# Band attention with a second pair of transposed weight tiles, a fourth row tile and a third query tile

## The chip, the cores and the metric

The kernel runs on one core of a Trainium2 chip. The time is the device time of one execution in microseconds, the median of three runs. A core has five engines that work side by side, each through its own queue in order: TensorE (PE, matmuls and transposes, with its weight loads shown apart as PEld), VectorE (DVE), ScalarE (ACT), GpSimd (POOL) and SyncE (SP), which here issues all the transfers. SBUF is the on-chip memory with 128 partitions, PSUM the banks that TensorE writes into.

## The reference

One step of a streaming encoder layer, on 2048 prompt tokens and 32 sample tokens of width 1024, in float32:

```
z = rmsnorm(x) @ w_in            # queries, keys, values of groups A and B
A: differential attention, 4 heads, two score maps each, all earlier chunks
B: band attention, 8 heads of 64: each 64-token chunk sees itself and 8 chunks before it
   s = q k^T / 8 + bias(head, distance); p = softmax(s); o = p v
h = x + concat(norm(A), norm(B)) @ w_out
h = h + relu(rmsnorm(h) @ w_up)^2 @ w_down
h = h + sigmoid(h @ w_ple_gate) * (p @ w_ple_proj)
y = rmsnorm(h)
```

The new keys and values are outputs too. The change concerns group B, the band attention.

## The kernel before

Every large product is made of three matmuls: each operand is split into a high part and a low part (`split`: a copy to the high part, and raw minus high for the low part), and `mm3` adds high x high, high x low and low x high. Weights come in units of 512 KB (`wunit`): one load (`wr`), a copy on ScalarE (`wh`, L169) and a subtraction on GpSimd (`wl`, L164).

The tokens are handled in four blocks of 512 (the last has the 32 sample tokens with it). In the order of the program `run` does: normalisation and group A's projections for blocks 0 and 1; group A's attention for their queries; group B's projections of blocks 0 and 1 with the normalisation of 2 and 3; band attention for the first 1024 queries; group B's projections of blocks 2 and 3; band attention for the other 1024 and the sample; group A's projections of blocks 2 and 3; group A's attention for those; and then, by blocks, output projection, MLP, gate and final normalisation. The order in which instructions really stand on each engine is not written out. The framework lays it out from priorities (program order, mostly) and a modelled time of each instruction. An instruction can be placed once its inputs are there and the tile that it writes has been released. So work from later in the program fills the holes of work before it: in the profile the projections of group A run within the first half of the band attention, and the output projection and MLP of block 0 within the second half.

A tile comes from a pool under a tag, with `bufs` copies. The tile of the next round waits until one copy has been released by its last reader. SBUF pools lie on two stacks, one from below (left), one from above (right). The band attention's pool `b` is on the right and is opened before its first half and closed after its second.

`attn_b` goes over four groups of query pairs, two in each half (`JB`), and in each over the eight heads. For each head and group it loads the head's bias (`bb`), keys (`kbt`) and values (`vbt`), each with two copies, and calls `attn_b_pair` for every pair of 128-query tiles, or for the sample's 32 queries (a visit, in what follows). One visit does, with L for a line of the kernel:

- `load_q`: two loads of 128 KB into the query tile `q` (two copies);
- for each of the two query tiles, scores `sb` in PSUM (L726) over up to 640 keys, bias and row maximum on VectorE into the row tile `eb` (tag `e`, three copies, L729; the small numbers are in `stb`), the exponential on ScalarE (L734), the reciprocal of the sum (L735), and the scaling on ScalarE (L736);
- transposes of the row tile into PSUM `tpb` (L741), a copy on ScalarE to the high part `pHb` (L750), and the low part `pLb` on VectorE (L751). Each holds both query tiles of the visit, and there is one copy of each;
- value matmuls `ob` (L766), the sum of the two halves of `ob` (L771 and L772), and the store to `oT`.

Three PSUM banks hold scores, two hold transposes, one holds the output.

Of the kernel before, what the change touches and what calls it, by code (L numbers as in the profile page):

```python
# [12 lines left out]
F32 = mybir.dt.float32  # L13
F32R = mybir.dt.float32r
# [5 lines left out]
P = 128  # L20
# [113 lines left out]
class Kern:  # L134
# [364 lines left out]

    def load_q(self, pool, gi, t0, n, maps):  # L500
        nc = self.nc
        q = pool.tile([P, len(maps), 2, 256], F32R, tag="q", bufs=2, name="q")
        for d in range(2):
            for i, m in enumerate(maps):
                self.dma(
                    q[64 * d : 64 * d + 64, i, :, :n],
                    self.qS[gi, :, 64 * m : 64 * m + 64, t0 : t0 + n].rearrange("l r c -> r l c"),
                )
        return q
# [182 lines left out]
    def attn_b_pair(self, h, j, kt, v, kb, bb, pool, ps_s, ps_t, ps_o):  # L692
        nc = self.nc
        gi, m = 4 + h // 2, h % 2
        samp = j is None
        if samp:
            tiles, t0, nq = [None], SP, SS
        else:
            tiles, t0, nq = [2 * j, 2 * j + 1], 256 * j, 256
        q = self.load_q(pool, gi, t0, nq, (m,))  # L700
        kfirst = 0 if samp else max(0, 2 * j - 4)
        pH = pool.tile([P, 6, 256], F32R, tag="pH", bufs=1, name="pHb")
        pL = pool.tile([P, 6, 256], F32R, tag="pL", bufs=1, name="pLb")
        spans = []
        for qi, t in enumerate(tiles):
            if samp:
                nr, k0, n, b0 = SS, SP, PAST + SS, 384
                kts = [(0, P), (1, SS)]
            else:
                nr = P  # L710
                f = max(0, t - 4)
                k0, n = P * f, P * (t + 1 - f)
                b0 = 640 - n
                kts = [(i, P) for i in range(f, t + 1)]
            spans.append(kts)
            if n <= 512:
                nb, w = 1, n
            else:
                nb, w = 2, n // 2
            e = pool.tile([P, 640], F32, tag="e", bufs=3, name="eb")[:nr, :n]  # L720
            st = pool.tile([P, 5], F32, tag="st", bufs=3, name="stb")[:nr]
            for i in range(nb):
                s = ps_s.tile([P, 512], F32, tag="s", name="sb")[:nr, :w]
                for hl in range(2):
                    c = k0 - kb + w * i
                    nc.tensor.matmul(  # L726
                        s, q[:, 0, hl, P * qi : P * qi + nr], kt[:, c : c + w], start=hl == 0, stop=hl == 1
                    )
                nc.vector.tensor_tensor_reduce(  # L729
                    e[:, w * i : w * i + w], s, bb[:nr, b0 + w * i : b0 + w * i + w], 1.0, -3e38,  # L730
                    ALU.add, ALU.max, st[:, 3 + i : 4 + i],
                )
            nc.vector.tensor_reduce(st[:, 0:1], st[:, 3 : 3 + nb], axis=AX.X, op=ALU.max, negate=True)
            nc.scalar.activation(e, e, AF.Exp, bias=st[:, 0:1], accum_out=st[:, 1:2])  # L734
            nc.vector.reciprocal(st[:, 2:3], st[:, 1:2])  # L735
            nc.scalar.activation(e, e, AF.Copy, scale=st[:, 2:3])  # L736
            for x0 in range(0, len(kts), 4):
                ch = kts[x0 : x0 + 4]
                tp = ps_t.tile([P, 4, P], F32, tag="tp", name="tpb")
                for x, (i, kn) in enumerate(ch):  # L740
                    nc.tensor.transpose(  # L741
                        tp[:kn, x, :nr], e[:, P * (x0 + x) : P * (x0 + x) + kn], self.ident[:nr, :nr]
                    )
                groups = [(0, len(ch), P)] if not samp else [(0, 1, P), (1, 1, SS)]
                for a0, na, kn in groups:
                    sl = ch[0][0] - kfirst + a0
                    h_ = pH[:kn, sl : sl + na, P * qi : P * qi + nr]
                    l_ = pL[:kn, sl : sl + na, P * qi : P * qi + nr]
                    s_ = tp[:kn, a0 : a0 + na, :nr]
                    nc.scalar.activation(h_, s_, AF.Copy)  # L750
                    nc.vector.tensor_tensor(l_, s_, h_.bitcast(F32), op=ALU.subtract)  # L751
        o = ps_o.tile([P, 256], F32, tag="o", name="ob")
        order = []
        if samp:
            order = [(0, P, 0, nq), (1, SS, 0, nq)]
        else:
            s0 = [i for i, _ in spans[0]]
            s1 = [i for i, _ in spans[1]]
            both = [i for i in s0 if i in s1]
            order = [(i, P, 0, 256) for i in both]  # L760
            order += [(i, P, 0, 128) for i in s0 if i not in s1]
            order += [(i, P, 128, 256) for i in s1 if i not in s0]
        for x, (i, kn, qa, qb) in enumerate(order):
            vt = v[:kn, (SP - kb) // P + i] if samp else v[:kn, i - kb // P]
            for y, pt in enumerate((pH, pL)):
                nc.tensor.matmul(  # L766
                    o[:, qa:qb], vt, pt[:kn, i - kfirst, qa:qb],
                    start=x == 0 and y == 0, stop=x == len(order) - 1 and y == 1,
                )
        t1 = pool.tile([64, 256], F32, tag="t1", bufs=2, name="t1")[:, :nq]  # L770
        nc.scalar.activation(t1, o[64:128, :nq], AF.Copy)  # L771
        nc.vector.tensor_tensor(t1, o[0:64, :nq], t1, op=ALU.add)  # L772
        self.dma(self.oT[64 * m : 64 * m + 64, gi, t0 : t0 + nq], t1)
# [532 lines left out]
```

## Time and profile before

| | |
|---|---|
| runs | 3271.13, 3277.6, 3279.51 us; median 3277.6 |
| profiled execution | 3282.74 us, its span 3281.0 us |
| mean granted TensorE clock | 0.974 |
| TensorE busy | 3096.6 us, 94% of the span |
| ScalarE, GpSimd, VectorE busy | 1696.1, 1711.0, 1562.2 us |
| memory traffic | 149 GB/s over the span |

How to read it: a row of a table of stages has, for a stretch of the span, the busy time of each engine with the count of its instructions, and then the clock that TensorE was granted (1.00 is full speed), the mean busy share of the 16 DMA engines, and what they moved in GB/s. A row of waits names who waited, for whom, the total in us, how often, and the longest. A row of instructions has line, engine, operation, output and inputs, shape and count, then busy time, the mean of one in ns, and the idle time of the engine before them with what ended it. Buffer numbers are left out of names. Some matmul records may be missing, and ends of matmuls are modelled.

### The profile page before, as it was taken

To read this page: it belongs to the slowest core of one execution; us is meant where nothing else is said; L and a number is where in the kernel's file an instruction comes from. 1 tells how busy PE (TensorE), PEld (TensorE's weight loads), DVE (VectorE), ACT (ScalarE), POOL (GpSimd) and SP (SyncE) were. 2 spreads that over 40 slices of the span, in tenths; PEclk is the share of its full clock that TensorE was granted. 3 is DMA by queue.
4 is the path that set the end of the run, shared out by engine and by line. 5 is a ranking of instruction groups with operands and counts; after the bars stand their busy time and mean duration, and the time that the engine had idled before them with its cause. 6 is when DMAs were issued, how large, how long until landed. Compare 5 with 4: busy or idle time off the path is not lost.

```text
span 3281.0 us, 51609 instructions
## 1 busy us (share of the span) xinstructions
PE 3096.6 (94%) x17881; PEld 2713.4 (83%) x17881; DVE 1562.2 (48%) x3952; ACT 1696.1 (52%) x3717; POOL 1711.0 (52%) x2515
## 2 busy tenths in 40 slices
PE   6998999899989999999999999998989999999998
PEld 6877788899877888778788877877779999999988
DVE  5116786444455544566655655735442232223235
ACT  4226676666656766666665656744442222222245
POOL 5436776433335544656654644676954333333377
PEclk9998999999999999999999999999989999999999
DMA  7488886876778654545655355357531111111123
GB/s 230 169 258 241 226 246 199 230 225 199 221 210 240 166 140 120 159 137 152 195 136 142 109 139 139 111 159 227 164 102 49 46 46 50 45 48 46 46 91 106
DMA packets 519085, 489.03 MB, mean 149 GB/s; under 512 B 37884, under 2 KB 414016, under 8 KB 518824
## 3 DMA queue, kind: packets, MB, share of 16 engines
q1 hardware_dynamic: 518824, 485.73, 50.8%
q8 instruction: 142, 2.33, 0.3%
q14 instruction: 119, 0.97, 0.1%
HBM read 379.06 MB, written 110.49 MB: 149 GB/s over the span
## 4 chain that ended last, share of the span: by engine, by line
PE 54%; DMA 5%; DVE 4%; POOL 2%; ACT 1%; issue 1%; SPq 0%; DVEq 0%; POOLq 0%; ACTq 0%
PE dps L190 7%; PE ups L191 7%; PE ups L190 7%; PE ups L192 7%; PE dps L192 7%; PE dps L191 7%; PE s L567 2%; PE gps L190 1%; PE gps L191 1%; DMA ka<-kS 1%; PE gps L192 1%; PE tpp L639 1%; POOL wl L164 1%; DMA wr<-w_up 1%; PE ob L766 1%
## 5 line engine op out<-in xcount | busy, mean ns | idle before, releaser
L164 POOL TENSOR_TENSOR wl<-wr,wh 128x256 fp32r<-128x256 f32 x936 | 690.9, 770 | 501.1 <-ACT wh L169 473.0
L971 DVE TENSOR_TENSOR h<-h,dps 128x512 f32<-128x512 f32 (+1 forms) x640 | 373.1, 585 | 597.5 <-PE dps L192 584.9
L169 ACT ACTIVATE wh<-wr 128x1024 fp32r<-128x1024 f32 x338 | 356.9, 1056 | 581.0 <-PE dps L191 285.7
L154 POOL TENSOR_TENSOR wl<-wr,wh 128x256 fp32r<-128x256 f32 x416 | 305.0, 764 | 407.0 <-ACT wh L169 403.7
L190 PE MATMUL dps<-uh,wh 128*128 128x512 f32 (+1 forms) x1280 | 458.6, 358 | 10.1 <-DVE h L971 5.5
L190 PE MATMUL ups<-cH,wh 128*128 128x512 f32 (+1 forms) x1280 | 453.3, 354 | 9.9 <-ACT relu L936 5.0
L191 PE MATMUL ups<-cL,wh 128*128 128x512 f32 (+1 forms) x1280 | 452.9, 354 | 4.1 <-DVE cL L175 3.6
L192 PE MATMUL ups<-cH,wl 128*128 128x512 f32 (+1 forms) x1280 | 453.2, 354 | 0.0
L191 PE MATMUL dps<-ul,wh 128*128 128x512 f32 (+1 forms) x1280 | 451.0, 353 | 0.0
L192 PE MATMUL dps<-uh,wl 128*128 128x512 f32 (+1 forms) x1280 | 450.9, 353 | 0.0
L154 POOL TENSOR_TENSOR ul<-relu,uh 128x136 fp32r<-128x136 f32 (+1 forms) x320 | 201.7, 652 | 167.7 <-ACT uh L169 166.4
L190 PEld LDWEIGHTS ups<-cH,wh 128*128 128x128 f32 x1280 | 242.8, 190 | 42.3 <-ACT relu L936 5.3
L190 PEld LDWEIGHTS dps<-uh,wh 128*128 128x128 f32 x1280 | 242.5, 189 | 42.4 <-DVE h L971 9.0
L191 PEld LDWEIGHTS ups<-cL,wh 128*128 128x128 f32 x1280 | 243.3, 190 | 36.0 <-DVE cL L175 3.8
L192 PEld LDWEIGHTS dps<-uh,wl 128*128 128x128 f32 x1280 | 242.0, 189 | 33.7
L192 PEld LDWEIGHTS ups<-cH,wl 128*128 128x128 f32 x1280 | 243.1, 190 | 30.1
L191 PEld LDWEIGHTS dps<-ul,wh 128*128 128x128 f32 x1280 | 242.2, 189 | 26.2
L190 PE MATMUL qps<-aH,wh 128*128 128x512 f32 (+1 forms) x640 | 231.3, 361 | 8.6 <-ACT kr L432 3.4
L191 PE MATMUL qps<-aL,wh 128*128 128x512 f32 (+1 forms) x640 | 229.6, 359 | 0.0
L192 PE MATMUL qps<-aH,wl 128*128 128x512 f32 (+1 forms) x640 | 228.9, 358 | 0.0
L567 PE MATMUL s<-ka,q 128*128 128x256 f32 (+4 forms) x784 | 190.4, 347 | 26.6 <-DMA ka<-kS 10.9
L581 ACT ACTIVATE e<-s,nm 128x512 f32<-128x512 f32 (+3 forms) x256 | 155.1, 611 | 68.7 <-DVE nm L573 46.0
(218 smaller groups left out, 7118.3 us busy)
## 6 DMA issues: line engine op xcount, KB each, us to landing
wr<-w_up SPq DMA_DIRECT2D x96, 512.0 KB, 4.2
wr<-w_down SPq DMA_DIRECT2D x96, 512.0 KB, 3.7
wr<-w_in SPq DMA_DIRECT2D x74, 512.0 KB, 5.2
q<-qS SPq DMA_DIRECT2D x256, 128.0 KB, 4.2
v<-vSa SPq DMA_DIRECT2D x64, 512.0 KB, 4.0
ka<-kS SPq DMA_DIRECT2D x32, 512.0 KB, 7.7
wr<-w_out SPq DMA_DIRECT2D x32, 512.0 KB, 5.4
wr<-w_ple_gate SPq DMA_DIRECT2D x32, 512.0 KB, 4.3
```

Of the source, the lines that this page charges most:

```text
L154: nc.gpsimd.tensor_tensor(out[:, sl], a[:, sl], b[:, sl], op=op)
L164: nc.gpsimd.tensor_tensor(out[:, sl], a[:, sl], b[:, sl], op=op)
L169: nc.scalar.activation(hi, raw, AF.Copy)
L190: nc.tensor.matmul(ps, lh, rh, start=start and i == 0, stop=False)
L191: nc.tensor.matmul(ps, lh, rl, start=False, stop=False)
L192: nc.tensor.matmul(ps, ll, rh, start=False, stop=stop and i == n - 1)
L567: nc.tensor.matmul(s, q[:, m, hl, P * qi : P * qi + nr], kt[:, m, k0 : k0 + n], start=hl == 0, stop=hl == 1)
L581: nc.scalar.activation(dst, src, AF.Exp, bias=nmx, accum_out=z[:nr, m, bi : bi + 1])
L639: nc.tensor.transpose(tp[:kn, x, :nr], w[:nr, P * i : P * i + kn], self.ident[:nr, :nr])
L766: nc.tensor.matmul(o[:, qa:qb], vt, pt[:kn, i - kfirst, qa:qb], start=x == 0 and y == 0, stop=x == len(order) - 1 and y == 1,)
L971: nc.vector.tensor_tensor(hv, hv, ps, op=ALU.add)
```

## The change

Four counts of tile copies and one size are changed; no instruction is added or taken away. In the band attention the query tile has three copies (in group A's attention, which passes two maps, it stays at two), `pHb` and `pLb` have two copies each, and `e` and `st` four. The program sets aside 1024 bytes of each SBUF partition for descriptors of dynamic DMAs, in place of the default 16384; they lie at address 0, below the left stack.

```diff
     def load_q(self, pool, gi, t0, n, maps):
         nc = self.nc
-        q = pool.tile([P, len(maps), 2, 256], F32R, tag="q", bufs=2, name="q")
+        q = pool.tile([P, len(maps), 2, 256], F32R, tag="q", bufs=4 - len(maps), name="q")
...
-        pH = pool.tile([P, 6, 256], F32R, tag="pH", bufs=1, name="pHb")
-        pL = pool.tile([P, 6, 256], F32R, tag="pL", bufs=1, name="pLb")
+        pH = pool.tile([P, 6, 256], F32R, tag="pH", bufs=2, name="pHb")
+        pL = pool.tile([P, 6, 256], F32R, tag="pL", bufs=2, name="pLb")
...
-            e = pool.tile([P, 640], F32, tag="e", bufs=3, name="eb")[:nr, :n]
-            st = pool.tile([P, 5], F32, tag="st", bufs=3, name="stb")[:nr]
+            e = pool.tile([P, 640], F32, tag="e", bufs=4, name="eb")[:nr, :n]
+            st = pool.tile([P, 5], F32, tag="st", bufs=4, name="stb")[:nr]
...
-    nc = bacc.Bacc("TRN2", target_bir_lowering=False, num_devices=1)
+    nc = bacc.Bacc("TRN2", target_bir_lowering=False, num_devices=1, dynamic_dma_scratch_size=1024)
```

## The prediction

> **What bounds the kernel now.** I read the page's busy times, its chain and its queues first, then a table by stages, then the waits inside the stage that the change touches. TensorE comes first on the page:
>
> ```profile
> PE 3096.6 (94%) x17881; PEld 2713.4 (83%) x17881; DVE 1562.2 (48%) x3952; ACT 1696.1 (52%) x3717; POOL 1711.0 (52%) x2515
> PE 54%; DMA 5%; DVE 4%; POOL 2%; ACT 1%; issue 1%; SPq 0%; DVEq 0%; POOLq 0%; ACTq 0%
> q1 hardware_dynamic: 518824, 485.73, 50.8%
> ```
>
> TensorE works for 3096.6 of 3281.0 us. The change adds and removes no instruction, so the TensorE work stays. What can move is its idle time, 184 us in all, and the clock it is granted. Band attention runs from 603 to 1330 us (its value matmuls, quoted further down). The stages, with the clock, the DMA share and GB/s in the last three columns:
>
> ```profile
> core 0: us, PE busy (x) PEld busy (x) DVE busy (x) ACT busy (x) POOL busy (x), PEclk, DMA share, GB/s
> 590.00:1340.00 750.00, 707.44 (x4282) 623.68 (x4281) 361.43 (x1237) 472.35 (x983) 307.04 (x486) 0.98 0.68 192
> 590.00:900.00 310.00, 289.90 (x2071) 271.38 (x2069) 141.65 (x548) 195.82 (x442) 101.44 (x182) 0.97 0.76 220
> 900.00:1000.00 100.00, 85.83 (x430) 70.95 (x431) 53.86 (x152) 61.98 (x118) 39.43 (x58) 0.93 0.75 210
> 1000.00:1340.00 340.00, 331.71 (x1782) 281.35 (x1781) 165.92 (x538) 214.56 (x424) 166.16 (x247) 1.00 0.58 162
> 300.00:500.00 200.00, 182.97 (x1088) 161.04 (x1086) 152.00 (x464) 136.49 (x391) 147.52 (x208) 0.94 0.82 230
> 200.00:250.00 50.00, 39.98 (x209) 33.54 (x209) 10.53 (x33) 13.48 (x29) 18.85 (x29) 0.89 1.03 320
> 2450.00:3100.00 650.00, 650.00 (x4038) 590.46 (x4037) 172.03 (x330) 182.69 (x316) 253.14 (x400) 1.00 0.15 46
> ```
>
> In the band stage, 590 to 1340 us, TensorE idles 750 - 707.4 = 42.6 us, and a clock of 0.98 costs about 15 us more (2% of 750): 57.6 us, 7.7% of the stage. Its parts differ: 20.1 us idle in the first half, 14.2 us in the hundred microseconds after it, 8.3 us in the last 340. The reason is the filler: projections in the first half, the MLP in the last, while after 900 us the projections have run out. The late MLP alone (2450 to 3100) keeps TensorE at 100%. So band attention is not slow work that stands in the way. It is a chain of small steps between which other work is fitted, and only the holes count. Which waits make them:
>
> ```profile
> PE sb L726 <- DVE stb L729: 10.4, 13, 3.6
> PE sb L726 <- DMA q<-qS: 5.9, 5, 1.8
> PE ob L766 <- ACT pHb L750: 4.6, 3, 2.3
> PE ops L190 <- DVE hd L860: 3.9, 2, 3.5
> PE tpb L741 <- DVE pLb L751: 1.7, 3, 0.8
> ```
>
> **What the single pair of weight tiles holds back.** One head of the second half, in which two pairs of query tiles and then the sample's 32 queries are done, from the time lines of ScalarE and TensorE (start, length, instruction):
>
> ```profile
> 1203.50 0.41 ACT L736 ACTIVATE eb<-eb,stb 32x160 f32<-32x160 f32 x1
> 1204.97 0.60 ACT L750 ACTIVATE pHb<-tpb 128x512 fp32r<-128x512 f32 x1
> ...
> 1218.68 0.27 PE L766 MATMUL ob<-pLb,vbt 128*128 128x128 f32 x1
> 1218.88 0.27 PE L741 MATMUL tpb<-ident,eb 32*128 32x32 f32 x2
> 1219.55 0.20 ACT L750 ACTIVATE pHb<-tpb 128x32 fp32r<-128x32 f32 x1
> ```
>
> The sample's row of 160 keys is scaled and ready at 1203.9 us. At 1205.0 a pair of prompt tiles begins to fill `pHb`, and its last value matmul ends at 1218.95. Only then is the sample transposed (1218.88) and copied (1219.55). It has waited 15 us, with one of three `e` tiles in its hands. With one `pHb`/`pLb` the pairs pass in single file, and the order in which the instructions are laid out puts filler between them.
>
> **The change, part by part.**
>
> Second `pHb`/`pLb` pair: the copies of one pair may run while the last one's value matmuls are pending. Waits at stake on TensorE: `ob` on `pHb` 4.6 and `tpb` on `pLb` 1.7 us. Bounds: from -6.3 (both go) to +6.3 (the copies queue on a busier ScalarE and both double). I take -4.6: the first goes, the second is a bank of PSUM, which the change leaves alone. Late next is the score bank (`sb` behind `stb`).
>
> Third query tile: two loads of 128 KB for each visit, started one visit earlier. No load is added.
>
> ```profile
> q<-qS SPq DMA_DIRECT2D x130, 128.0 KB, 3.7
> SPq L145 <- PE sb L726: 35.6, 23, 4.7
> SPq L145 <- POOL wl L164: 42.4, 24, 6.0
> ```
>
> SP, which issues every transfer in order, stood 35.6 us behind `sb` matmuls that still read a query tile or keys, and all later loads, the weight loads among them, stood behind it. A landing takes 3.7 us, less than a visit (a band of 727 us over 64 pairs and 8 sample visits, 10 us). So the 5.9 us that TensorE waited for queries should go: -5.9, with 0 as the other end if SP is held by `wl` (42.4 us, which the change doesn't touch).
>
> Fourth `e` and `st`: two prompt pairs hold four. Waits at stake are `sb` behind `stb`, 10.4 us; this is VectorE draining score banks, of which there are three as before. From -10.4 to +10.4; I take 0, because a tile for the result doesn't free a bank.
>
> The gap from 900 to 1000 us: 14.2 us idle, 3.6 and 3.5 us of it in the two longest single waits above. With more rows in flight, attention can fill part of it. Bounds 0 and -14.2; I take a third, -5.
>
> Scratch: 15,360 bytes of each partition come free at address 0, the left-hand pools slide down by that, and 2,048 + 2 x 6,144 + 2,560 + 20 = 16,916 bytes are taken on the right. No instruction hangs on it; the work that would show a cost is the next stage's start, whose tiles lie where the band pool lay, before as after: 0. [...]
>
> Clock: 15 us lost against 42.6 idle is 0.35 us for each idle microsecond. 4.6 + 5.9 + 5 = 15.5 less idle gives -5.5. Bounds 0 and -15. [...]
>
> What denser attention costs: first, how far ScalarE lets it be denser. Two rows for the instructions on `eb` on ScalarE, one for those on `pHb` on all engines, and the groups of the output:
>
> ```profile
> 590.00:900.00 310.00, 100.85 (x207) 0.97 0.76 220
> 900.00:1340.00 440.00, 109.54 (x201) 0.98 0.62 173
> 603.00:1330.00 727.00, 88.87 (x352) 68.84 (x352) 104.17 (x238) 91.29 (x238) 0.98 0.67 191
> L771 ACT ACTIVATE t<-ob 64x256 f32<-64x256 f32 x64 | 24.4, 381 | 40.7 <-PE ob L766 37.8 <-DMA q<-qS 1.7
> L766 PE MATMUL ob<-pHb,vbt x352: 178/281/562, 603.3 to 1329.8; 128*128 128x256 f32 x120, 128*128 128x128 f32 x48, 128*128 128x32 f32 x8
> ```
>
> ScalarE's part is 100.85 + 109.54 on `eb`, 91.29 (the fourth time of the third row) on `pHb`, and 24.4 for the output: 210.4 + 91.3 + 24.4 = 326 us of ScalarE for attention, in a band of 727 us, and 472 with the filler's. If nothing but ScalarE held it, the band would take 472 us. I take the middle of 727 and 472, 600 us. Filler displaced from it runs later, where it costs TensorE its own time and no more (2450 to 3100). But in a denser stage TensorE waits oftener: from 300 to 500 us, with VectorE at 76% and ScalarE at 68%, it loses 17.0 us idle and 12 us of clock, 14.5%. I charge +8 us, about a quarter, since VectorE is the slacker engine here, between 0 and the +30 that the rival below works out.
>
> Sum: -4.6 - 5.9 - 5 - 5.5 + 8 = -13 us. The profiled execution took 3282.7 us (3281.0 span and 1.7 around it), 5.1 above the median of 3277.6. It becomes 3269.7, and the median 3264.6: 3265 us.
>
> **The rivals.**
>
> Slower, by density. The stage is 600 us long and loses at the rate of 300 to 500 us: 600 x 14.5% = 87 us, against 57.6 now: +30, 3308 us. It decides from 57.6 / 600 = 9.6% on. For it: the last 340 us lose only 2.4% in idle while ScalarE runs at 63%; there is hardly anything to win there and much to lose. Against it: from 300 to 500 VectorE was the busier engine, and the band leaves VectorE at 48%. Chance 0.31.
>
> Slower, by transfers. The first half moves 220 GB/s at a DMA share of 0.76. Packed from 310 into 250 us it needs 0.94. At 1.03 (200 to 250 us) TensorE idled 20%. A hundred microseconds of that are 20 us, less the 6.5 those lose now: +14, 3292 us. It decides once the share passes that of 300 to 500 us, 0.82, for long. Chance 0.08.
>
> Slower, by the scratch. The page calls the queue dynamic, and if its descriptors did lie in the scratch, transfers would land later, a query tile say as late as the slowest loads on the page:
>
> ```profile
> ka<-kS SPq DMA_DIRECT2D x32, 512.0 KB, 7.7
> ```
>
> That is 4.0 us more for each landing. TensorE's five waits for queries would grow by 5 x 4.0 = 20 us: 3298. It decides from about 3 us more per landing. Chance 0.03.
>
> No change to be measured: TensorE is full, and what attention gives up filler takes. Within 0.3% (10 us, about what a measurement here tells from nothing): 3278. Chance 0.10.
>
> **How the numbers follow.** Forecast 0.48; so faster 0.48, same 0.10, slower 0.31 + 0.08 + 0.03 = 0.42. The forecast's own range is 3240 to 3268. The low end of the whole range takes the idle 42.6 us and 5 us of clock away: 3230. The high end is the density rival at 650 us, 94 - 57.6 = +37: 3315.
>
> **What would show it.** Right: the last `ob` ends near 1200 us, not 1330; the copies into `pHb` begin before the last pair's value matmuls end; TensorE's waits for queries are nearly gone; the sample's row no longer waits 15 us; the next attention stage starts and ends earlier by as much; TensorE's idle total falls from 184 to about 170 us. The density rival would show ScalarE above 75% in the band with more `sb` behind `stb`; the transfers, waits for `kbt`, `vbt`, `bb` with the share above 0.9. What makes it wrong: a new order of instructions that opens holes elsewhere, above all where the MLP ends and the output projection starts.

## The result, and the profile after

The changed kernel takes 3262.46 us (median of 19 runs, 3251.43 to 3271.29), the kernel before 3278.56 us beside it (19 runs, 3270.78 to 3292.62). The ratio is 0.9948, with a 95% interval of 0.9937 to 0.9958: faster by 0.5%, some 17 us. The profiled execution took 3256.5 us, 6 us less than the median, and the profiled one of before was 4 us above its own. So the spans of the two profiles, 3281.0 and 3254.6 us, lie 26 us apart, about 10 us of which is chance.

The page's lines on busy time and on the chain, after:

```profile
PE 3076.7 (95%) x17881; PEld 2692.7 (83%) x17881; DVE 1557.3 (48%) x3952; ACT 1693.7 (52%) x3717; POOL 1706.8 (52%) x2515
PE 26%; DVE 1%; ACT 0%; issue 0%; DVEq 0%; POOL 0%; POOLq 0%
```

The counts of instructions are the same. TensorE's idle time is 3254.6 - 3076.7 = 177.9 us, 6.5 less than before's 184.4.

The table of stages, after, with the same columns as in the prediction:

```profile
590.00:1340.00 750.00, 714.95 (x4361) 627.76 (x4360) 392.91 (x1309) 494.78 (x1055) 306.54 (x484) 0.99 0.69 197
590.00:900.00 310.00, 289.83 (x2082) 268.00 (x2081) 154.80 (x615) 211.98 (x479) 90.92 (x169) 0.99 0.77 223
900.00:1000.00 100.00, 94.13 (x538) 80.64 (x537) 60.20 (x169) 65.46 (x129) 47.10 (x69) 0.98 0.84 242
1000.00:1340.00 340.00, 330.99 (x1745) 279.12 (x1745) 177.90 (x527) 217.35 (x448) 168.51 (x248) 0.99 0.58 160
2450.00:3100.00 650.00, 650.00 (x4040) 590.07 (x4039) 179.07 (x344) 179.99 (x310) 251.84 (x397) 1.00 0.16 48
```

The late MLP is as full as it was. The band stage idles 35.0 us in place of 42.6. All of that is the hundred microseconds after 900: 5.9 idle, down from 14.2. The first half (590 to 900 us: 20.2 against 20.1) and the last 340 us (9.0 against 8.3) have not gained. But the first half isn't unchanged inside. The same stretch in two parts, first before, then after:

```profile
590.00:700.00 110.00, 96.68 (x709) 92.24 (x708) 51.75 (x215) 72.24 (x186) 33.36 (x67) 0.94 0.82 239
700.00:900.00 200.00, 193.22 (x1365) 179.14 (x1362) 89.90 (x333) 123.58 (x257) 68.08 (x115) 0.99 0.72 209
```

```profile
590.00:700.00 110.00, 91.12 (x630) 80.38 (x629) 66.84 (x278) 89.78 (x225) 29.19 (x63) 0.97 0.89 248
700.00:900.00 200.00, 198.71 (x1454) 187.61 (x1453) 87.97 (x337) 122.19 (x254) 61.73 (x106) 1.00 0.71 210
```

Until 700 us attention now comes so thick that ScalarE is busy 89.78 of 110 us (82%, before 66%), and TensorE idles 18.9 us in place of 13.3. After that the filler that was passed over makes it up: 1.3 us idle in place of 6.8. Where the filler has gone, the projections' last matmuls and the band's value matmuls show, first before (the row of the value matmuls stands in the prediction), then after:

```profile
L190 PE MATMUL qps<-aH,wh x640: 282/390/796, 87.9 to 891.0; 128*128 128x512 f32 x96, 128*128 128x272 f32 x64
```

```profile
L190 PE MATMUL qps<-aH,wh x640: 282/390/795, 87.8 to 919.5; 128*128 128x512 f32 x96, 128*128 128x272 f32 x64
L766 PE MATMUL ob<-pHb,vbt x352: 177/280/415, 600.5 to 1258.9; 128*128 128x256 f32 x120, 128*128 128x128 f32 x48, 128*128 128x32 f32 x8
```

The projections end 28 us later, the band attention 71 us earlier. What stands in the hole after 900 us is seen by TensorE's work on one tile there: the projections' `qps` after (none before), and the output projection's `ops` before and after:

```profile
900.00:1000.00 100.00, 13.55 (x96) 0.98 0.84 242
900.00:1000.00 100.00, 56.44 (x220) 0.93 0.75 210
900.00:1000.00 100.00, 53.82 (x213) 0.98 0.84 242
```

So left-over projections fill it. TensorE's waits in the band stage, after:

```profile
PE sb L726 <- DVE stb L729: 9.5, 18, 1.4
PE sb L726 <- DMA q<-qS: 5.6, 5, 2.7
PE ob L766 <- ACT pHb L750: 3.6, 4, 1.5
```

The waits that the change was to take away, for queries (5.9 before) and for `pHb` (4.6 before), are nearly as long as they were. Another profile of the order of before, that of the smaller scratch alone, has 7.9 and 3.7 us, so differences of a microsecond or two are chance.

The other part of the gain is the granted clock. Over the 19 runs its mean was 0.980, which is 65 us of clock lost in an execution; the kernel before, in the runs beside the experiments, lost 73 to 76 us (24 to 35 runs on each of three chips, mean 0.977 to 0.978). About 6.5 us of idle and 8 to 11 us of clock make the 17 us. How much of the clock comes from the band stage isn't shown: in the two profiles it differs as well until 590 us, ahead of the band attention (0.96 and 0.97). Idle times are from one profile each, and the profile of the kernel with the smaller scratch alone has 189.6 us where before's has 184.4: a few microseconds of them are chance.

### The profile page after: what moved, and what is told of

Its sections match the earlier page's. It is cut to its first block, busy times and chain, and to the rows that moved or that the text cites. A ratio compares the mean times of both kernels' runs of the same rounds, so it can differ in the third digit from the quotient of the medians.

```text
span 3254.6 us, 51557 instructions
## 1 busy us (share of the span) xinstructions
PE 3076.7 (95%) x17881; PEld 2692.7 (83%) x17881; DVE 1557.3 (48%) x3952; ACT 1693.7 (52%) x3717; POOL 1706.8 (52%) x2515
```

## The experiments

Each was timed in five rounds against the kernel before (5 to 12 runs of it, 24 to 35 of before). The ratios, with what one profile of each shows (idle time of TensorE between 590 and 1340 us, and when the band's last value matmul ended):

| kernel | ratio | 95% interval | idle, us | band ends, us |
|---|---|---|---|---|
| before | 1 | | 42.6 | 1330 |
| scratch alone | 0.9996 | 0.9984 to 1.0008 | 40.2 | 1330 |
| + pair | 0.9956 | 0.9936 to 0.9976 | 38.1 | 1295 |
| + row | 0.9993 | 0.9982 to 1.0005 | 42.5 | 1303 |
| + query | 0.9963 | 0.9949 to 0.9978 | 33.5 | 1307 |
| + row, query | 0.9983 | 0.9974 to 0.9992 | 43.1 | 1315 |
| + pair, row | 0.9989 | 0.9976 to 1.0002 | 36.7 | 1261 |
| + pair, query | 0.9971 | 0.9957 to 0.9986 | 30.2 | 1265 |
| + pair, row, query (the change) | 0.9948 | 0.9937 to 0.9958 | 35.0 | 1259 |
| the change, first half alone | 1.0019 | 1.0008 to 1.0030 | 45.2 | 1311 |
| the change, second half alone | 1.0059 | 1.0047 to 1.0071 | 49.0 | 1326 |
| the change, a pool for each half | 0.9991 | 0.9977 to 1.0005 | 35.7 | 1281 |
| the change, bias loaded last | 0.9998 | 0.9987 to 1.0010 | 43.1 | 1261 |
| the change, row 5, query 4 | 0.9989 | 0.9977 to 1.0001 | 44.6 | 1274 |

**One part at a time.** The scratch alone:

```diff
-    nc = bacc.Bacc("TRN2", target_bir_lowering=False, num_devices=1)
+    nc = bacc.Bacc("TRN2", target_bir_lowering=False, num_devices=1, dynamic_dma_scratch_size=1024)
```

> The kernel before with the 1024 bytes of scratch alone. The order of instructions on every engine is that of before; only addresses move. All theories but one: ratio 1.000 (0.998 to 1.002), granted clock as before's one profile, 0.974 to 0.980. Theory that the scratch itself costs or gives time: outside that band. It also serves as a second set of clocks for the order of before.

It does nothing to the time that can be measured: 0.9996. The order of instructions is line for line that of before. What it does is room: without it the three counts together don't fit, since the pool `wq` needs 21.25 KB of each partition and 17.06 are left.

With it, each count by itself:

```diff
-        pH = pool.tile([P, 6, 256], F32R, tag="pH", bufs=1, name="pHb")
-        pL = pool.tile([P, 6, 256], F32R, tag="pL", bufs=1, name="pLb")
+        pH = pool.tile([P, 6, 256], F32R, tag="pH", bufs=2, name="pHb")
+        pL = pool.tile([P, 6, 256], F32R, tag="pL", bufs=2, name="pLb")
```

> Before, with the scratch and the second pHb/pLb pair alone (row tiles 3, query tiles 2). Theory 'single file' (the one pair of weight tiles sets the pace): most of the 16 us of the whole change, 0.995 to 0.997, band end near 1260 us. Theory 'row tiles' (the score rows are what runs out): 0.998 to 1.000, band end near 1320. Theory 'any new order' (what counts is where holes happen to fall): anywhere from 0.993 to 1.005 with no relation to the band's end.

```diff
-            e = pool.tile([P, 640], F32, tag="e", bufs=3, name="eb")[:nr, :n]
-            st = pool.tile([P, 5], F32, tag="st", bufs=3, name="stb")[:nr]
+            e = pool.tile([P, 640], F32, tag="e", bufs=4, name="eb")[:nr, :n]
+            st = pool.tile([P, 5], F32, tag="st", bufs=4, name="stb")[:nr]
```

> Before, with the scratch and the fourth row tile (e and st) alone. Theory 'single file': 0.999 to 1.001, band end near 1330, since the fourth row waits for the one pair of weight tiles. Theory 'row tiles': 0.995 to 0.997, band end near 1260. Theory 'any new order': anywhere from 0.993 to 1.005.

```diff
-        q = pool.tile([P, len(maps), 2, 256], F32R, tag="q", bufs=2, name="q")
+        q = pool.tile([P, len(maps), 2, 256], F32R, tag="q", bufs=4 - len(maps), name="q")
```

> Before, with the scratch and the third query tile alone. Prediction's term: TensorE's 5.9 us of waits for queries go, 0.998. Theory that the query tile is not what the loads wait for (the waits stayed at 5.6 us in the changed kernel): 1.000 with the waits still 4 to 7 us. Theory 'any new order': anywhere from 0.993 to 1.005.

The pair gives 0.9956, the query tile 0.9963, the row tile nothing that can be measured. The pair came out as 'single file' has it, in the time; its band ends 35 us earlier, half of what that theory said. The query tile gave more than the prediction's whole term (5.9 us would be 0.998). In its profile the waits for queries did shrink, to

```profile
PE sb L726 <- DMA q<-qS: 3.1, 3, 1.5
PE s L567 <- DMA q<-qS: 3.1, 1, 3.1
```

but the second line is a new wait of group A's, whose matmuls already run here, so the sum hardly moved. Its gain lies in the hole after 900 us, as in the whole change:

```profile
900.00:1000.00 100.00, 91.21 (x528) 79.74 (x528) 58.68 (x162) 64.30 (x125) 48.13 (x71) 0.98 0.84 240
```

That gave the theory 'gap': any of these tiles lets attention run ahead in the first half, leaves projections over, and so fills that hole once. It says that pair and query tile don't add up. With the query tile 96 matmuls on `qps` do stand after 900 us. With the pair none does (the last begins at 896.7), and its hole, 8.6 us idle, is filled by more of the output projection, TensorE on `ops`:

```profile
900.00:1000.00 100.00, 68.09 (x270) 0.98 0.81 236
```

So one hole is filled by two kinds of work. Over their runs the pair alone and the query tile alone lose 73 us of clock in an execution, and before beside them 76. Their profiles have 176 and 175 us of idle time, against 184 and 190 in the two of the order of before: most of their gain is idle time, by one profile each.

**One part taken out again.** The changed kernel with one of its counts at the old value:

```diff
-        pH = pool.tile([P, 6, 256], F32R, tag="pH", bufs=2, name="pHb")
-        pL = pool.tile([P, 6, 256], F32R, tag="pL", bufs=2, name="pLb")
+        pH = pool.tile([P, 6, 256], F32R, tag="pH", bufs=1, name="pHb")
+        pL = pool.tile([P, 6, 256], F32R, tag="pL", bufs=1, name="pLb")
```

> The changed kernel with one pHb/pLb pair again (row 4, query 3, scratch 1024). Theory 'single file' (the pair sets the pace): back to 0.998 to 1.000. Theory 'gap' (whatever puts more visits in flight fills the hole behind the projections, 900 to 1000 us, once; so pair and query tile do the same job and don't add up): 0.995 to 0.997, as the query tile alone.

```diff
-        q = pool.tile([P, len(maps), 2, 256], F32R, tag="q", bufs=4 - len(maps), name="q")
+        q = pool.tile([P, len(maps), 2, 256], F32R, tag="q", bufs=2, name="q")
```

> The changed kernel with two query tiles again (pair 2, row 4). Theory 'single file': 0.995 to 0.996, the query tile adds nothing. Theory 'gap': 0.994 to 0.997, as the pair alone. Theory 'queries early' (the loads one visit ahead are what counts): 0.998 to 1.000.

```diff
-            e = pool.tile([P, 640], F32, tag="e", bufs=4, name="eb")[:nr, :n]
-            st = pool.tile([P, 5], F32, tag="st", bufs=4, name="stb")[:nr]
+            e = pool.tile([P, 640], F32, tag="e", bufs=3, name="eb")[:nr, :n]
+            st = pool.tile([P, 5], F32, tag="st", bufs=3, name="stb")[:nr]
```

> The changed kernel with three row tiles (pair 2, query 3, scratch 1024). So far: pair alone 0.9956, query alone 0.9963, row alone 0.9993, pair and row 0.9989, row and query 0.9983, all three 0.9948. Theory 'each count has its own price': pair times query, 0.992. Theory 'gap' (both fill one hole): 0.995 to 0.996. Theory 'any new order': anywhere from 0.993 to 1.001; none of the three gives a number here.

Any two are worth less than the three (0.9983, 0.9989, 0.9971 against 0.9948; the intervals of the third and of the change just touch, the others are clear of it), and by the medians adding the row tile, which is worth nothing alone, takes the gain of the pair from 0.9956 to 0.9989 and of the query tile from 0.9963 to 0.9983, but improves that of both. Those three steps are within or at the edge of the intervals, so none of them is shown. The intervals allow less than the medians say: the change can't be told from the pair alone or the query tile alone, and is clear of the scratch, of the row tile, and of the two kernels with the row tile and one other. No price for each count gives such a table: pair times query tile would be 0.992, and is 0.9971. 'Single file' had the kernel without the pair (0.9983) and not that without the query tile (0.9989), 'queries early' the second and not the pair alone (0.9956); both fall. So does 'gap' in its simple form, which had 0.995 to 0.997 for the kernel without the pair: with row and query tile the hole after 900 us is closed too (5.3 us idle), and the gain is a third.

**One half at a time.** `attn_b_pair` takes its counts from a number that is set before each half, and the second half has a pool of its own:

```diff
+            self.deep = 1          # first half: 1; second half: 0 (and the other way round)
             for js in JB[: len(JB) // 2]:
                 self.attn_b(js, bp, ps_s, ps_t, ps_o)
...
+            bx.close()
+            bx = ExitStack()
+            bp = opened(bx, "b2", 1, side="right")
+            self.deep = 0
             wqx = ExitStack()
```

> All of the change's tiles in the first half of the band attention alone; the second half has a pool of its own with the old counts. Theory 'gap': the hole after 900 us lies in the second half, so it stays, and the first 100 us lose up to 10 us to density: 0.999 to 1.003. Theory 'pace' (the band's end comes earlier and that is the gain): half of it, 0.997.

> All of the change's tiles in the second half alone. Theory 'gap': the hole after 900 us is filled and nothing is lost before 700 us: 0.993 to 0.996, as good as the whole change or better. Theory 'pace': half of the gain, 0.997.

Both are slower than before; the first lies where 'gap' had it, and the second is 0.6% slower where 'gap' and 'pace' had it faster. But the edit does more than it says, since the second pool's tiles wait for the first pool's. So the same with the change's counts in both halves:

> All of the change's tiles in both halves, the second half with a pool of its own: the control for the two runs with one half deep. If the second pool itself costs (its tiles wait for those of the first half at the same addresses), 1.001 to 1.006, with the hole behind 840 us open; if it costs nothing, as the whole change, 0.993 to 0.996, and the two half runs can be read as they stand.

0.9991 in place of 0.9948, between the two expectations: the second pool alone costs about 0.4%, and the two runs with one half can't be read for what each half is worth. In the run with the second half deep the seam is seen in the stages, and in what TensorE waited for in all of the band:

```profile
700.00:900.00 200.00, 181.24 (x1247) 168.53 (x1246) 82.82 (x306) 114.83 (x236) 63.75 (x107) 0.96 0.67 192
900.00:1000.00 100.00, 88.83 (x429) 74.15 (x428) 53.67 (x148) 61.05 (x114) 37.65 (x58) 0.89 0.79 228
```

```profile
PE sb L726 <- DMA q<-qS: 12.6, 3, 8.4
```

One wait of 8.4 us for a query tile stands there, in a stretch that idles 18.8 us in place of 6.8. The first half's last value matmul begins at 876.4 us, the second half's first bias load at 878.1, and its first value matmul at 904.9. A pool boundary between two loops that used to overlap is a wait for the attention. Whether TensorE idles in it is another matter. The run with the change's counts in both pools has the same seam, 31 us without a value matmul from 845.3 us on, and no such hole:

```profile
700.00:900.00 200.00, 196.67 (x1438) 185.95 (x1437) 83.82 (x316) 117.26 (x245) 66.67 (x112) 0.99 0.72 208
900.00:1000.00 100.00, 96.14 (x551) 83.04 (x550) 59.54 (x167) 66.19 (x128) 44.68 (x68) 0.98 0.84 244
```

There TensorE has projections to work on until 925 us; with the second half alone deep they end at 879. And the band stage of the run with both pools deep idles 35.7 us, as little as the change's, so its 0.4% (14 us) isn't lost there. Its clock (71 us lost, 65 in the change) and the idle time outside the band (148.0 us in its profile, 142.9 in the change's) make 11 us of it.

**Another order of the same work.** The tiles of the change, and each head's bias loaded after its keys and values:

```diff
-            bb = self.bias_b(pool, h)
             kt = pool.tile([P, KBW], F32R, tag="kb", bufs=2, name="kbt")
...
+            bb = self.bias_b(pool, h)
             for j in js:
                 self.attn_b_pair(h, j if j < 8 else None, kt, v, kb, bb, pool, ps_s, ps_t, ps_o)
```

> The changed kernel with each head's bias loaded after its keys and values in place of before. Same tiles, same instructions, another order. Theory 'the counts did it': 0.994 to 0.996, as the change. Theory 'any new order': off by more than 0.002 from it, either way.

0.9998: the whole gain is gone, with every tile of the change in place and the band ending at 1261 us, as in the change. The parts of its band stage:

```profile
590.00:700.00 110.00, 89.59 (x647) 79.84 (x646) 66.78 (x279) 88.99 (x225) 30.06 (x67) 1.00 0.90 253
700.00:900.00 200.00, 195.24 (x1408) 183.61 (x1408) 83.73 (x319) 117.32 (x245) 60.30 (x104) 0.99 0.70 204
900.00:1000.00 100.00, 94.68 (x562) 83.83 (x561) 63.12 (x179) 69.54 (x134) 45.40 (x68) 0.98 0.85 246
1000.00:1340.00 340.00, 327.35 (x1712) 278.43 (x1711) 181.17 (x539) 218.23 (x458) 168.28 (x244) 0.97 0.57 159
```

The thick start is there (20.4 us idle until 700), the hole after 900 is filled (5.3), but the two stretches beside them idle 4.8 and 12.6 us where the change has 1.3 and 9.0. That is 43.1 us in all, as before. It isn't that scores wait for the later bias: VectorE's waits for it at L729, 4.1 us in the change, aren't there in this run. GpSimd, which masks the bias, does stand longer for it (124 us; 98 in the change, 112 before); whether that costs anything isn't shown.

**More of the same.**

```diff
-            e = pool.tile([P, 640], F32, tag="e", bufs=4, name="eb")[:nr, :n]
-            st = pool.tile([P, 5], F32, tag="st", bufs=4, name="stb")[:nr]
+            e = pool.tile([P, 640], F32, tag="e", bufs=5, name="eb")[:nr, :n]
+            st = pool.tile([P, 5], F32, tag="st", bufs=5, name="stb")[:nr]
...
-        q = pool.tile([P, len(maps), 2, 256], F32R, tag="q", bufs=4 - len(maps), name="q")
+        q = pool.tile([P, len(maps), 2, 256], F32R, tag="q", bufs=6 - 2 * len(maps), name="q")
```

> The changed kernel with one more of each, five row tiles and four query tiles (the pair stays at two, for lack of room). Theory 'pace': faster still, 0.992 to 0.994. Theory 'density' (ScalarE at 84% from 600 to 700 us is too much already): 0.996 to 1.000.

0.9989, as 'density' has it. Its first stretch loses more to clock and idle than any other:

```profile
590.00:700.00 110.00, 89.24 (x569) 78.11 (x567) 58.51 (x257) 80.97 (x205) 24.13 (x56) 0.89 0.85 233
```

**What follows.** Over the fourteen kernels, time goes with the idle time of the band stage (correlation 0.77; 1.3 us of time for 1 us of idle). Loosely: without the run with the second half deep it is 0.68 and 0.9 us, and the least idle band, 30.2 us with pair and query tile, isn't the fastest kernel. It doesn't go with the pace: four kernels end the band between 1259 and 1265 us, and their ratios are 0.9948, 0.9989, 0.9971 and 0.9998. By stretches, TensorE's idle time in microseconds is:

| kernel | 590 to 700 | 700 to 900 | 900 to 1000 | 1000 to 1340 |
|---|---|---|---|---|
| before | 13.3 | 6.8 | 14.2 | 8.3 |
| + pair, query | 13.3 | 2.8 | 7.4 | 6.8 |
| + row | 21.0 | 1.0 | 5.3 | 15.2 |
| the change | 18.9 | 1.3 | 5.9 | 9.0 |
| the change, bias loaded last | 20.4 | 4.8 | 5.3 | 12.6 |

Pair and query tile fill the hole after 900 us part way (8.6 and 8.8 us idle, one at a time) and leave the first stretch nearly as it was (14.4 and 14.8). The fourth row tile fills the hole further, to between 3.2 and 5.9 us in every kernel that has it in both halves, and makes the first stretch worse: 18.2 to 21.0 us idle in each of the eight kernels that have it in the first half, 5 to 8 more than before. With the row tile alone the two cancel. ScalarE's load doesn't say which: with pair and query tile it is busy 84.15 of the first 110 us and TensorE idles 13.3, with row and query tile 78.91 and 20.7. Idle time isn't all of the loss there, since the clock in that stretch went from 0.88 (pair and query tile) to 1.00 (bias last), by one profile each. What is left over depends on how the rest of the order falls, and a swap of one load moves it by 0.5%. Of the seven kernels with the fourth row tile in both halves the change alone gains more than 0.2%: its order is a lucky one among these neighbours. The pair alone and the query tile alone, without a fourth row tile, can't be told from it in time. Why this order falls well in the last 340 us and that with the bias last doesn't, the runs don't show.

## Why the prediction was right or wrong

The time (3265 forecast, 3262.5 measured), the sign and the range held. The sum of terms was right by luck, with errors that cancelled: for pair, query tile, gap, clock and density it had -4.6, -5.9, -5, -5.5 and +8 us, and the runs show about -1, 0, -8, -8 to -11 and 0. The waits of which the first two were made are still there. Point by point:

- *Pair, -4.6.* The wait for `pHb` went from 4.6 to 3.6 us. The step that failed is the single file. With two copies it is still a file. The sample's row in the changed kernel, from the time lines of ScalarE, VectorE and TensorE:

```profile
1166.31 0.43 ACT L736 ACTIVATE eb<-eb,stb 32x160 f32<-32x160 f32 x1 [0.64 <-DVE stb L735]
...
1169.54 0.58 ACT L750 ACTIVATE pHb<-tpb 128x512 fp32r<-128x512 f32 x1
1172.16 0.22 PE L766 MATMUL ob<-pLb,vbt 128*128 128x128 f32 x1
1177.75 0.29 DVE L751 TENSOR_TENSOR pLb<-tpb,pHb 128x128 fp32r<-128x128 f32 x1
...
1182.50 0.27 PE L766 MATMUL ob<-pLb,vbt 128*128 128x128 f32 x1
1182.70 0.53 PE L741 MATMUL tpb<-ident,eb 32*128 32x32 f32 x3
1183.21 0.20 ACT L750 ACTIVATE pHb<-tpb 128x32 fp32r<-128x32 f32 x1
```

  The copies now overlap: those of the pair ahead of the sample begin (1169.5) before the last value matmul of the pair before that (1172.2). But the sample's row, ready at 1166.7, is transposed at 1182.7: it still waits 16 us, until the value matmuls of the pair ahead of it have ended. From 1172.4 one copy of `pHb` and `pLb` was free, and at 1178.0 the last transposes ahead of it had been read. For the last 4.7 us no tile held it back: it stood in the place that the laid-out order gave it, behind filler and the pair's value matmuls. The transposes write `tpb`; the one pair of weight tiles could hold back only the copies behind them.
- *Query tile, -5.9.* 5.6 of the 5.9 us remain. The other end named for it, 0, is what happened. SP still stands as long behind `sb` (35.6 before), and nearly so behind `wl` (39.0, 42.4 before), the cause named for that end; which of the two keeps the queries late isn't shown:

```profile
SPq L145 <- PE sb L726: 36.7, 22, 6.0
```

- *Row tile, 0.* Right alone (0.9993). Together with the others its medians go in either direction, within what the intervals leave open.
- *The gap, -5.* Right in place, too small: -8.3. It was filled by projections that had been passed over (96 matmuls on `qps`, 13.6 us), not by more rows in flight as the step said: the same stretch has 430 and 538 matmuls, and without those 96 nearly the same number (442).
- *Scratch, 0.* Right: 0.9996 (0.9984 to 1.0008) for the scratch alone.
- *Clock, -5.5.* 8 to 11 us, by the means over the runs.
- *Density, +8.* The place was right: 5.6 us more idle until 700 us, with ScalarE at 82%; the reason is in doubt, since pair and query tile alone bring ScalarE to 77% there without any more idle (though with a clock of 0.88 in that profile, before 0.94). It was regained between 700 and 900 (5.5 us), so the first half paid nothing. The band's length was put at 600 us and is 659 (600.5 to 1259).
- *Signs.* The last `ob` begins at 1259 us, half way to the 1200 named; group A's next attention ends 65 us earlier (2055 against 2120 us); the idle total is 177.9, not 170. The waits for queries and the sample's 16 us, the two signs that belong to removed waits, failed.
- *Rivals.* The loss that density named is there, with the fourth row tile and not with ScalarE's load: of the eight kernels that have it in the first half, all but the change are within 0.2% of before. Two kernels of the family are slower beyond their interval, the first half alone (1.0019) and the second alone (1.0059), the latter with the seam of its pools. Transfers: the share rose to 0.89 until 700 us without new waits on keys or values among TensorE's longest. Scratch: no.

## What to carry to other kernels

Where the order of instructions is laid out by a model, a larger count of buffers is a new order first and a removed wait second: look whether the waits that it was to remove are gone, and time a neutral reordering beside it before the buffers get the credit. Where one engine is nearly full (TensorE here, 94 to 95% of the span), a faster side chain need not gain anything by itself: here four kernels with the same pace differ by 0.5%. In these runs the time went with the holes, if loosely (correlation 0.77), and they are found by a table of stages, not by the pace of the chain. Packing a side chain early can leave filler for a hole later; in these runs that was worth up to the 14 us of the hole, less what the packed stretch idled.

## What the runs showed of the hardware

In the profile of before the granted clock falls also where there is no long pause. Between 590 and 900 us no single wait of TensorE was longer than 2.3 us, and yet the clock was halved three times before 700 us. The three, each with the stretch ahead of it, in the table by windows with the columns of the stage tables:

```profile
624.60:628.00 3.40, 1.20 (x7) 0.91 (x7) 1.21 (x4) 3.38 (x9) 2.44 (x4) 1.00 1.15 266
628.00:631.40 3.40, 3.31 (x15) 3.34 (x16) 0.52 (x2) 2.10 (x5) 1.55 (x5) 0.50 0.95 270
645.10:648.50 3.40, 1.11 (x9) 1.06 (x9) 1.08 (x2) 2.76 (x4) 1.60 (x3) 1.00 0.63 193
648.50:651.90 3.40, 3.40 (x17) 3.40 (x16) 1.66 (x9) 3.35 (x9) 3.40 (x6) 0.50 0.81 230
655.30:658.70 3.40, 0.85 (x4) 0.33 (x2) 1.87 (x8) 3.35 (x8) 2.36 (x4) 1.00 1.03 274
658.70:665.50 6.80, 5.98 (x27) 6.01 (x28) 0.33 (x2) 2.52 (x7) 0.70 (x3) 0.50 0.56 186
```

Ahead of each, TensorE worked 1.20, 1.11 and 0.85 us of 3.40, in pieces; then, for 3.4, 3.4 and 6.8 us in which it was busy nearly throughout, it had half its clock. So these three halvings came behind several short waits in a row, none of them longer than 2.3 us. Over the whole of this execution, from 45 to 3260 us, the clock was halved 28 times, each time with 0 to 2.4 us of TensorE work in the 3.4 us ahead (the shortest stretch in the trace's record of the clock), and each full-speed stretch of 3.4 us, counted in step with the halvings, that held less than 1.6 us of work was followed by one. Ahead of two of the halvings, at 303.7 and 351.5 us, no pause was longer than 0.9 us. Of the stretches with 1.6 to 2.4 us some were followed by one and some weren't. In the changed kernel's profile a stretch with 1.48 us, from 2316.5 us, had another 3.4 us at full speed behind it, without any work, before the clock was halved: 1.6 us is what one execution showed. The clock also goes with the scatter between runs of one kernel: over the changed kernel's 19 runs time and granted clock have a correlation of -0.75, and executions differ by 20 us (3251.43 to 3271.29) with the same instructions in the same order. Which of the two moves the other isn't shown.
